# Four of the six modulation parts of each layer, computed ahead of that layer's own attention heads instead of in the layer before it and in the attention stage

## The chip, the cores and the metric

The kernel runs on one core of one Trainium2 chip, as one program. The metric is the device time of one execution in microseconds (us). A core has five engines that work side by side, each through its own queue in a fixed order: the tensor engine (PE: matmuls, with the weight loads shown apart as PEld), VectorE (DVE), ScalarE (ACT), GpSimd (POOL) and SyncE (SP), which issues every DMA transfer of this kernel. Results of PE land in PSUM banks, from which VectorE or ScalarE must take them before the bank can be used again.

## The reference, cut to what matters

Two layers of a decoder trunk over 1024 tokens of width 1024. Each layer has a mixing part (two attention branches, each of eight heads, merged by gates) and an MLP. A conditioning vector `c` gives each layer six vectors of 1024 numbers: shift, scale and gate of the mixing part, and shift, scale and gate of the MLP.

```python
c_act = jax.nn.silu(c)
for l in range(DEPTH):
    mod = (c_act @ w_ada[l] + b_ada[l])[:, None, :]
    shift1, scale1, gate1, shift2, scale2, gate2 = jnp.split(mod, N_MOD, axis=-1)
    h = _rms_norm(x, g_mix_norm[l]) * (1.0 + scale1) + shift1
    p = h @ w_in[l]
    ...
    x = x + gate1 * (merged @ w_mix_out[l])
    h = _rms_norm(x, g_mlp_norm[l]) * (1.0 + scale2) + shift2
    x = x + gate2 * (jnp.square(jax.nn.relu(h @ w_up[l])) @ w_down[l])
return _rms_norm(x, g_final)
```

`w_ada[l]` is 1024 x 6144 in f32: 24 MB for each layer, 4 MB for each of the six parts. Parts 0 and 1 (shift1, scale1) are needed at the start of the layer; part 2 (gate1) only when the merged attention output is added to x, parts 3 and 4 at the norm of the MLP, and part 5 at its end.

## The kernel before

Every f32 product is made of three matmuls on operands split into a rounded part and a rest (`hi`, `lo`): ScalarE casts the weight tile (`raw` to `parts`, `pr` to `pw`, `wr` to `ws`), GpSimd subtracts, and PE multiplies. A layer goes through these stages:

- The **front** (first part of `layer`): the norm of x, the latent projections, their norm (`lat_norm`) and rotary tables; then the projections of the first q, k, v and the first gates out of `hh`/`hl` (tiles `H`), and for p in 0 to 3 the head projections out of the latents (`lath`/`latl`, tiles `lh` and `ll`), with weights from `q_parts` and `kv_parts`. `linear` yields after each half of a job: 24 matmuls into one PSUM bank `pp`, or 9 and 6 in the head projections. There are four `pp` banks here.
- **Attention** (`attend`, two `pp` banks): eight heads of each branch, interleaved with the remaining projections (`fill`).
- The **merge**, the mixing output and the norm of the MLP.
- The **up product** (tiles `b`, `t` by weights `pw`): 14 steps of a loop over m, with seven products each, after four plain jobs.
- The **down product** (tiles `bo` by weights `ws`) in `down`, 56 steps, whose end overlaps the norm of the next layer.

The modulation sums (`modulation`) multiply c with `w_ada`. A part is four chunks of 256 columns. For each chunk four transfers of 256 KB go into the two buffers `AD`, VectorE makes eight multiply-and-add instructions into `A` (`mac`), ScalarE casts, GpSimd subtracts, and PE adds over the partitions by four matmuls of two columns (`tp<-const,A`), after which VectorE adds the bias. `modulation` is a generator: each `next` puts one transfer and two VectorE instructions in the program, so that the sums are spread over other work.

What a place in the program means is decided by `Plan`: all operations are recorded, PE's in the order of the code, and each gets a due time from PE's order; `schedule` then lays out all five queues by due time, buffers that are free, and durations that it reckons itself. The result is a fixed order for each engine. Buffers are given in turn (`AD` has two, `A` three), and a transfer that waits for its buffer holds up the transfers behind it in SyncE's queue.

Of the kernel before, what the change touches and what calls it, by code (L numbers as in the profile page):

```python
# [25 lines left out]
DEPTH = 2  # L26
# [20 lines left out]
def bc(ap):  # L47
    return ap.bitcast(F32)
# [440 lines left out]
class Trunk:  # L489
# [633 lines left out]
    def layer(self, l, xT, ssq, before):  # L1123
# [9 lines left out]
        def qkv(p):  # L1133
            qd[p], kd[p], vd[p] = self.two(), self.two(), self.dt([P, S])
            return [
                (win_w(p * P), self.keep_split(qd[p]), P),
                (win_w(512 + p * P), self.keep_split(kd[p]), P),
                (win_w(1024 + p * P), self.keep(vd[p]), P),
            ]

        def gate(m):
            gd[m] = self.dt([P, S])
            return (win_w(2208 + m * P), self.keep(gd[m], AF.Sigmoid if m < 8 else AF.Copy), P)
# [23 lines left out]
        def rope(ps, sl, n, out):  # L1167

            a, b = ltmp(), ltmp()
            nc.vector.tensor_mul(a, ps, cos[:, sl])  # L1170
            nc.vector.tensor_mul(b[:64], ps[64:], sin[64:, sl])
            nc.vector.tensor_mul(b[64:], ps[:64], sin[:64, sl])
            nc.vector.tensor_add(a, a, b)
            hi, lo = ltmp(F32R), ltmp(F32R)
            nc.scalar.copy(out=hi, in_=a)
            nc.vector.tensor_sub(lo, a, bc(hi))
            for i, t in enumerate((hi, lo)):
                for r in (0, 64) if n < 64 else (0,):
                    m = n if n < 64 else P
                    o = r // 64 * n  # L1180
                    nc.sync.dma_start(out=out[i, o : o + m, sl], in_=bc(t[r : r + m]))
# [10 lines left out]
        def lat_norm(b, tiles, width, g):  # L1192
            for hf, sl in enumerate(HALVES):
                R = self.rstd(acc[b, hf], width, ltmp)
                for i in tiles:
                    t = raw[i][:, sl]
                    nc.vector.scalar_tensor_tensor(
                        out=t, in0=t, scalar=self.v(l, g, 1, i - tiles[0]), in1=R, op0=ALU.mult, op1=ALU.mult
                    )
                    nc.scalar.copy(out=lath[i][:, sl], in_=t)  # L1200
                    nc.vector.tensor_sub(latl[i][:, sl], t, bc(lath[i][:, sl]))
# [36 lines left out]
        lat_norm(0, range(0, 3), QR, "g_q_lat")  # L1238
        lat_norm(1, range(3, 5), KVR, "g_kv_lat")
        kr_job = (kr_w, lambda ps, sl: rope(ps, sl, 16, kpe_d), P)  # L1240
        for _ in self.linear([kr_job] + qkv(0) + [gate(m) for m in range(4)], hh, hl, KT):
            pass

        c_qp, c_lt = self.vcls("qp", 16, 17, *range(18, 24)), self.vcls("lt2", 15, 5, 6, 7)

# [15 lines left out]
        def q_parts(g):  # L1261
            groups = ((0, 64), (64, 80), (80, 96))
            r = []
            for k0, k1 in ((0, 2), (2, 3)):
                r += by_heads(I["w_q_up"], k0, k1, g * 4 * QK_DIM, 4, QK_DIM, groups, c_qp)
            return r

        def kv_parts(p):
            return by_heads(I["w_kv_up"], 0, 2, 256 * p, 2, P, ((0, 64), (64, 128)), self.W["parts"])

        part = lambda w, c: lambda: [tuple(t[:, c : c + P] for t in k) for k in w]
        for p in range(4):
            mq[p], mk[p], mv[p] = self.two(), self.two(), self.dt([P, S])
            if p % 2 == 0:
                wq = q_parts(p // 2)
            q_w = part(wq, p % 2 * P)
            for _ in self.linear([(q_w, self.keep_split(mq[p], ltmp), P)], lath, latl, 3):
                pass
            wkv = kv_parts(p)
            k_w, v_w = part(wkv, 0), part(wkv, P)  # L1280
            kv_jobs = [(k_w, self.keep_split(mk[p], ltmp), P), (v_w, self.keep(mv[p]), P)]
            for _ in self.linear(kv_jobs, lath[3:], latl[3:], 2):
                pass
            if p % 2 == 0:
                g = p // 2
                qr_d[g] = self.two()
                w = part(wq, 2 * P)()
                for sl in HALVES:
                    ps = self.bank("pp")
                    self.mm3(ps, w, lath, latl, sl, 3)  # L1290
                    rope(ps, sl, 64, qr_d[g])
            for _ in self.linear([gate(4 + p)], hh, hl, KT):
                pass

        self.attention_banks()

# [67 lines left out]
        fill = [self.linear(qkv(p + 1), hh, hl, KT) for p in range(3)]  # L1364
        fill += [self.linear([gate(m) for m in range(8, 16)], hh, hl, KT)]
        fill = self.chain(fill)
        ada = self.modulation(0, [2, 3, 4, 5]) if l == 0 else iter(())
        for name, head, weights, mask, vals, steps in (
            ("sb", sb_head, self.sb_weights, self.mask_s, vd, SB_STEPS),
            ("mla", mla_head, self.mla_weights, self.mask_c, mv, MLA_STEPS),  # L1370
        ):
            if name == "sb":
                self.c_q, self.c_F = self.vcls("sq", *q_slots[:6]), self.vcls("F", *q_slots[6:])
            else:
                self.c_q = self.vcls("mq", *q_slots)
                fill = self.chain([fill, sb_out()])
            for p in range(4):
                od[name, p] = self.dt([P, S])
                a = self.attend([head(p, e) for e in range(2)], lambda: self.make_v(vals[p]), weights, mask, od[name, p])
                self.interleave(a, 19, fill, steps[p], ada)  # L1380
        for _ in self.chain([fill, ada]):
            pass


# [38 lines left out]
        steps = self.linear([(mix_w(m), update(m, 16, ssq), P) for m in range(KT)], mh, ml, KT, halves_first=True)  # L1423
# [22 lines left out]

        NP = DFF // P // 2
        hid = [self.dt([P, 8, HALF]) for m in range(NP)]
        ada = self.modulation(l + 1, range(6)) if l + 1 < DEPTH else iter(())

        def hidden(f):
            where = (0, 7) if f % 2 == 0 else (1, 2)
# [23 lines left out]
        for m in range(2, DFF // P // 2):  # L1476
            a, S3, c, d, S1, S2, S4 = self.pair_weights(I["w_up"][l, :, 2 * m * P : 2 * (m + 1) * P], c_pr, c_pw)
            u, v = self.full(c_u), self.full(c_u)
            next(ada, None)
            p1 = self.product(a, B11)  # L1480
            nc.scalar.copy(out=u[:, :HALF], in_=p1)
            p6 = self.product(S2, T[2])
            nc.vector.tensor_add(u[:, HALF:], p6, u[:, :HALF])
            next(ada, None)
            p7 = self.product(S3, T[3])
            nc.vector.tensor_add(v[:, :HALF], p7, u[:, HALF:])
            p5 = self.product(S1, T[1])
            nc.vector.tensor_add(v[:, HALF:], p5, v[:, :HALF])
            nc.vector.tensor_add(u[:, HALF:], p5, u[:, HALF:])
            next(ada, None)  # L1490
            p4 = self.product(d, T[4])
            nc.vector.tensor_sub(v[:, :HALF], v[:, :HALF], p4)
            p2 = self.product(c, B21)
            nc.vector.tensor_add(u[:, :HALF], p2, u[:, :HALF])
            next(ada, None)
            p3 = self.product(S4, B22)
            nc.vector.tensor_add(u[:, HALF:], p3, u[:, HALF:])
            for t in (v, u):
                nc.scalar.activation(out=t, in_=t, func=AF.Relu)
                nc.scalar.activation(out=t, in_=t, func=AF.Square)  # L1500
            nc.sync.dma_start(out=hid[m][:, 0], in_=u[:, :HALF])
            nc.sync.dma_start(out=hid[m][:, 1:3], in_=v.rearrange("p (a b) -> p a b", a=2))
            combine(m, u, v)
            if m in (3, 5):
                u, v = self.full(c_u), self.full(c_u)
                i = m // 2 - 1
                nc.sync.dma_start(out=u[:, :HALF], in_=hid[i][:, 0])
                nc.sync.dma_start(out=u[:, HALF:], in_=hid[i][:, 7])
                nc.sync.dma_start(out=v.rearrange("p (a b) -> p a b", a=2), in_=hid[i][:, 1:3])
                combine(i, u, v)  # L1510
        ssq = [self.tmp(), self.tmp()]
        steps = self.down(l, hid, x_d, ssq)
        for _ in range(48):
            next(steps)
            next(ada, None)
        for _ in ada:
            pass
        return self.xT, ssq, steps

    def down(self, l, hid, x_d, ssq):  # L1520
# [111 lines left out]
            yield from g  # L1632

    @staticmethod
    def interleave(a, na, b, nb, c):

        done = 0
        for i, _ in enumerate(a):
            if i % 2 == 1:
                next(c, None)  # L1640
            want = (i + 1) * nb // na
            while done < want:
                next(b, None)
                done += 1
# [69 lines left out]
```

## Time and profile before

| | |
|---|---|
| median of 3 runs | 3286.44 us (3281.02 to 3287.44) |
| the profiled execution, its own time | 3293.0 us |
| its span, first to last instruction | 3291.2 us |
| PE busy | 94% of the span |
| VectorE, ScalarE, GpSimd busy | 69%, 47%, 37% |
| mean granted clock of PE | 0.98 |

The profile is that of one execution. A busy share is an average over stages with different limits. A row of a window gives the busy time of each engine in that stretch, with the number of its instructions; the granted clock is a share of the full 2.4 GHz.

### The profile page before, as it was taken

What the parts mean: (1) busy time and instruction counts of PE and PEld (TensorE: products, weight loads), DVE (VectorE), ACT (ScalarE), POOL (GpSimd) and SP (SyncE); (2) the same over time, 40 slices, a digit from 0 to 9 for tenths busy, and PEclk for the clock granted to TensorE, in tenths of its full rate; (3) what the DMA queues carried; (4) which work ended last, traced back from release to release, by engine and by line L of the source; (5) the groups of instructions that cost most, each with busy time, mean ns of one, the idle gap of its engine ahead of it and who ended that gap; (6) DMA issues with size and microseconds to landing.
All of it is one profiled execution on the core that took longest, in us unless ns stands there. A gap on an engine that the chain in (4) does not pass through costs nothing. (4 is left out here: it accounts for less than half of the span.)

```text
span 3291.2 us, 42785 instructions
## 1 busy us (share of the span) xinstructions
PE 3103.3 (94%) x14823; PEld 2510.8 (76%) x14823; DVE 2258.7 (69%) x3238; ACT 1544.9 (47%) x2643; POOL 1229.2 (37%) x952
## 2 busy tenths in 40 slices
PE   5999999999998898999989999999999989999998
PEld 4877777788776776777777877778887767888786
DVE  7453677678667778799986225656766777558886
ACT  4443555566444443433344225666654444444334
POOL 3222444111244544345433223441113455544442
PEclk9999999999999999999999999999999999999999
DMA  6446456555843654876332474444466435467522
GB/s 219 151 146 202 136 151 164 140 139 171 271 140 103 200 194 161 281 226 199 99 122 76 139 221 125 130 117 124 101 213 208 141 114 196 154 226 225 179 77 90
DMA packets 450268, 532.45 MB, mean 162 GB/s; under 512 B 32498, under 2 KB 320900, under 8 KB 450052
## 3 DMA queue, kind: packets, MB, share of 16 engines
q1 hardware_dynamic: 450052, 529.72, 52.7%
q8 instruction: 117, 1.92, 0.3%
q14 instruction: 99, 0.81, 0.1%
HBM read 367.60 MB, written 162.00 MB: 161 GB/s over the span
## 5 line engine op out<-in xcount | busy, mean ns | idle before, releaser
L213 PE MATMUL pp<-H,parts 128*128 128x512 f32 x4032 | 1060.2, 407 | 10.5 <-ACT H L213 8.9
L213 PEld LDWEIGHTS pp<-H,parts 128*128 128x128 f32 x4032 | 741.0, 191 | 162.7 <-ACT H L213 10.4
L213 PE MATMUL pp<-bo,ws 128*128 128x512 f32 x2688 | 645.6, 401 | 31.3 <-POOL ws L213 15.0
L213 POOL TENSOR_TENSOR parts<-raw,parts 128x1024 fp32r<-128x1024 f32 (+2 forms) x168 | 370.7, 2208 | 721.2 <-ACT parts L213 681.5
L213 PEld LDWEIGHTS pp<-bo,ws 128*128 128x128 f32 x2688 | 508.4, 191 | 155.5 <-POOL ws L213 18.1
L213 POOL TENSOR_TENSOR ws<-wr,ws 128x1024 fp32r<-128x1024 f32 x112 | 297.1, 2662 | 368.7 <-ACT ws L213 342.0
L213 PE MATMUL pp<-t,pw 128*128 128x512 f32 x1344 | 323.4, 398 | 10.7 <-ACT u L213 10.0
L213 PEld LDWEIGHTS pp<-t,pw 128*128 128x128 f32 x1344 | 251.5, 189 | 71.8 <-ACT u L213 11.2
L213 ACT CAST parts<-raw 128x1024 fp32r<-128x1024 f32 (+2 forms) x168 | 151.9, 904 | 242.1 <-PE pp L213 202.2
L213 PE MATMUL pp<-b,pw 128*128 128x512 f32 x1008 | 246.8, 402 | 12.4 <-DVE u L213 12.4
L213 DVE TENSOR_TENSOR wtl<-tp,wth 128x512 fp32r<-128x512 f32 (+3 forms) x384 | 207.0, 550 | 67.3 <-ACT wth L213 65.6
L213 DVE SCALAR_TENSOR_TENSOR A<-AD,const,A 128x256 f32<-128x256 f32 x280 | 223.3, 797 | 26.6 <-DMA AD<-in_w_ada 23.2
L213 POOL TENSOR_TENSOR pw<-T,pw 128x512 fp32r<-128x512 f32 x112 | 162.3, 1464 | 208.4 <-ACT pw L213 194.4
L213 ACT CAST wth<-tp 128x512 fp32r<-128x512 f32 (+3 forms) x384 | 181.1, 481 | 125.2 <-PE tp L213 120.5
L213 DVE TENSOR_TENSOR_SCAN F<-F,sc 128x128 f32<-128x128 f32 (+7 forms) x128 | 171.7, 1349 | 99.1 <-ACT F L213 74.2
L213 DVE SCALAR_TENSOR_TENSOR x<-pp,const,x 128x512 f32<-128x512 f32 x256 | 181.7, 741 | 80.0 <-PE pp L213 80.0
L213 PEld LDWEIGHTS pp<-b,pw 128*128 128x128 f32 x1008 | 190.4, 191 | 59.5 <-DVE u L213 14.8
L213 POOL TENSOR_TENSOR W<-W,F 128x127 f32<-128x127 f32 (+7 forms) x128 | 155.2, 1217 | 209.7 <-ACT W L213 122.8
L213 ACT CAST bo<-T 128x512 fp32r<-128x512 f32 x224 | 135.3, 619 | 185.8 <-DMA T<-dram 124.4
L213 DVE TENSOR_TENSOR bo<-T,bo 128x512 fp32r<-128x512 f32 x224 | 201.4, 946 | 18.3 <-ACT bo L213 17.9
L213 PE MATMUL tp<-const,W 128*128 128x128 f32 x1152 | 185.1, 274 | 17.8 <-DVE wtl L213 9.8
L213 ACT ACTIVATE u<-u 128x1024 f32<-128x1024 f32 x112 | 118.7, 1060 | 149.1 <-DVE u L213 142.6
(151 smaller groups left out, 4620.6 us busy)
## 6 DMA issues: line engine op xcount, KB each, us to landing
T<-dram SPq DMA_DIRECT2D x352, 256.0 KB
dram<-T SPq DMA_DIRECT2D x208, 256.0 KB
dram<-u SPq DMA_DIRECT2D x92, 512.0 KB
AD<-in_w_ada SPq DMA_DIRECT2D x160, 256.0 KB
raw<-in_w_in SPq DMA_DIRECT2D x70, 512.0 KB
wr<-in_w_down SPq DMA_DIRECT2D x64, 512.0 KB
pr<-in_w_up SPq DMA_DIRECT2D x56, 512.0 KB
sq<-dram SPq DMA_DIRECT2D x96, 256.0 KB
```

The source lines that it names most:

```text
L213: getattr(getattr(nc, engine), method)(*[r(x) for x in a], **{n: r(x) for n, x in k.items()})
```

## The change

Parts 2 to 5 of layer 0 were spread over layer 0's attention, and all six parts of layer 1 over layer 0's up and down products. Now parts 2 to 5 of each layer are spread over that layer's own front, from the q, k, v projections to the last head projection; parts 0 and 1 of layer 1 stay in layer 0's up product, and the attention stages and the down product have none. In the up product there are now three `next` calls in each step in place of four.

```diff
@@ -1238,8 +1238,10 @@
+        ada = self.modulation(l, [2, 3, 4, 5])
         for _ in self.linear([kr_job] + qkv(0) + [gate(m) for m in range(4)], hh, hl, KT):
-            pass
+            next(ada, None)
+            next(ada, None)
...
             for _ in self.linear([(q_w, self.keep_split(mq[p], ltmp), P)], lath, latl, 3):
-                pass
+                next(ada, None)
...
             for _ in self.linear(kv_jobs, lath[3:], latl[3:], 2):
-                pass
+                next(ada, None)
...
                     rope(ps, sl, 64, qr_d[g])
+                    next(ada, None)
             for _ in self.linear([gate(4 + p)], hh, hl, KT):
-                pass
+                next(ada, None)
+                next(ada, None)
+        for _ in ada:
+            pass
...
-        ada = self.modulation(0, [2, 3, 4, 5]) if l == 0 else iter(())
...
-                self.interleave(a, 19, fill, steps[p], ada)
-        for _ in self.chain([fill, ada]):
+                self.interleave(a, 19, fill, steps[p])
+        for _ in fill:
             pass
...
-        ada = self.modulation(l + 1, range(6)) if l + 1 < DEPTH else iter(())
+        ada = self.modulation(l + 1, range(2)) if l + 1 < DEPTH else iter(())
...
-            next(ada, None)
             p4 = self.product(d, T[4])
...
+        for _ in ada:
+            pass
         for _ in range(48):
             next(steps)
-            next(ada, None)
-        for _ in ada:
-            pass
```

What this does to the queues is shown at three places.

First, VectorE's queue in layer 0's front, at the head projections of p = 0. `lt<-pp,lt` takes the rest of a q or k projection out of its bank, `lt<-pp,cs` is the start of the rotary step. Before:

```order
L213 TENSOR_TENSOR lt_319_1690<-pp_1668,lt_318_1685 128x512
L213 TENSOR_TENSOR lt_322_1708<-pp_1683,lt_321_1703 128x512
L213 TENSOR_TENSOR lt_328_1735<-pp_1701,lt_327_1717 128x512
L213 TENSOR_TENSOR lt_331_1751<-pp_1713,lt_330_1742 128x512
L213 TENSOR_TENSOR lt_338_1773<-pp_1749,cs_1184 128x512
```

And of the change:

```order
L213 TENSOR_TENSOR lt_380_1805<-pp_1774,lt_379_1793 128x512
L213 SCALAR_TENSOR_TENSOR A_1748<-AD_1770,const_98,A_1748 128x256
L213 TENSOR_TENSOR lt_387_1822<-pp_1791,lt_386_1815 128x512
L213 TENSOR_SCALAR A_1836<-AD_1796,const_98 128x256
L213 SCALAR_TENSOR_TENSOR A_1836<-AD_1796,const_98,A_1836 128x256
L213 TENSOR_TENSOR const_277<-tp_1828,const_252 128x2
L213 SCALAR_TENSOR_TENSOR A_1836<-AD_1830,const_98,A_1836 128x256 x2
L213 TENSOR_TENSOR lt_395_1871<-pp_1813,lt_394_1838 128x512
L213 SCALAR_TENSOR_TENSOR A_1836<-AD_1854,const_98,A_1836 128x256 x2
L213 TENSOR_TENSOR lt_399_1899<-pp_1832,lt_398_1882 128x512
L213 TENSOR_TENSOR lt_413_1908<-pp_1877,cs_1184 128x512
```

The five evacuations of PSUM banks, which followed each other, now have one to four instructions of the sums between them, each of which waits for its own transfer into `AD`.

Second, VectorE's queue in layer 0's down product. `x<-pp,const,x` adds a product to x, `wr` forms a weight combination. Before:

```order
L213 SCALAR_TENSOR_TENSOR A_13085<-AD_12968,const_98,A_13085 128x256
L213 TENSOR_TENSOR wr_12839<-wr_12413,wr_12839 128x1024
L213 SCALAR_TENSOR_TENSOR A_13085<-AD_13112,const_98,A_13085 128x256
L213 SCALAR_TENSOR_TENSOR x_12563<-pp_13114,const_277,x_12563 128x512
L213 SCALAR_TENSOR_TENSOR A_13085<-AD_13112,const_98,A_13085 128x256
L213 SCALAR_TENSOR_TENSOR x_12563<-pp_13114,const_277,x_12563 128x512
L213 SCALAR_TENSOR_TENSOR A_13085<-AD_13147,const_98,A_13085 128x256
L213 SCALAR_TENSOR_TENSOR x_12756<-pp_13114,const_277,x_12756 128x512
```

And of the change:

```order
L213 SCALAR_TENSOR_TENSOR x_12308<-pp_12864,const_277,x_12308 128x512 x2
L213 SCALAR_TENSOR_TENSOR x_12494<-pp_12864,const_277,x_12494 128x512 x2
L213 TENSOR_TENSOR wr_12586<-wr_12279,wr_12586 128x1024
L213 TENSOR_TENSOR wr_12427<-wr_12427,wr_12586 128x1024
L213 SCALAR_TENSOR_TENSOR x_12378<-pp_12897,const_277,x_12378 128x512 x2
```

The evacuations now follow each other without the sums between them.

Third, SyncE's queue in layer 0's front, around the loads of the head projections' weights (`raw<-in_w_kv_up`). Before:

```order
L213 DMA raw_1567<-in_w_kv_up 128x2x256
L213 DMA raw_1577<-in_w_in 128x8x128
L213 DMA dram_1585<-T_1572 128x512
L213 DMA dram_1585<-T_1606 128x512
L213 DMA raw_1621<-in_w_kv_up 128x2x256
```

And of the change:

```order
L213 DMA raw_1605<-in_w_kv_up 128x2x256
L213 DMA AD_1612<-in_w_ada 128x2x256
L213 DMA raw_1624<-in_w_in 128x8x128
L213 DMA AD_1635<-in_w_ada 128x2x256
L213 DMA dram_1581<-lt_1622 16x512 x2
L213 DMA dram_1581<-lt_1630 16x512
L213 DMA AD_1654<-in_w_ada 128x2x256
L213 DMA dram_1581<-lt_1630 16x512
L213 DMA dram_1671<-T_1616 128x512
L213 DMA AD_1685<-in_w_ada 128x2x256
L213 DMA dram_1671<-T_1675 128x512
L213 DMA raw_1697<-in_w_kv_up 128x2x256
```

Four transfers of the sums now stand between two weight loads and the stores of the projections.

Counted over the whole order, the groups of four small matmuls stand before: 16 in layer 0's attention, 13 in its up product, 11 in its down product. After: 14 in layer 0's front (the first 568 other matmuls ahead of the first score) and 2 just behind the first score, over 630 matmuls; 8 in its up product, one for every 112 other matmuls where it was one for every 84; and 16 in layer 1's front, over 635 matmuls. In both up and down products the order of PE's other matmuls stays as it was.

## Rows read from the trace of the kernel before

**Rows 1.** Page, busy us of each engine, share of the span, instructions.

```profile
PE 3103.3 (94%) x14823; PEld 2510.8 (76%) x14823; DVE 2258.7 (69%) x3238; ACT 1544.9 (47%) x2643; POOL 1229.2 (37%) x952
```

**Rows 2.** Tiles' PE instructions: count, ns min/median/max, first and last start in us.

```profile
L213 PE MATMUL sc<-sq,sq x192: 274/390/776, 304.6 to 570.1; 128*128 128x512 f32 x96, 128*128 128x256 f32 x64, 128*128 128x384 f32 x32
L213 PE MATMUL pp<-merged,parts x384: 388/394/503, 893.9 to 989.2; 128*128 128x512 f32 x192
L213 PE MATMUL pp<-b,pw x504: 387/395/797, 1051.2 to 1361.3; 128*128 128x512 f32 x168
...
L213 PE MATMUL sc<-sq,sq x192: 274/390/509, 1967.3 to 2220.1; 128*128 128x512 f32 x96, 128*128 128x256 f32 x64, 128*128 128x384 f32 x32
L213 PE MATMUL pp<-merged,parts x384: 387/394/499, 2523.9 to 2615.9; 128*128 128x512 f32 x192
L213 PE MATMUL pp<-b,pw x504: 387/394/400, 2678.6 to 2953.3; 128*128 128x512 f32 x168
```

**Rows 3.** Windows, both layers: busy PE, PEld, DVE, ACT, POOL; clock, DMA share, GB/s.

```profile
304.60:893.90 589.30, 556.12 (x3153) 456.26 (x3152) 418.36 (x786) 339.48 (x690) 173.50 (x235) 0.99 0.59 167
1967.30:2523.90 556.60, 540.23 (x3089) 447.48 (x3088) 354.27 (x648) 336.04 (x676) 162.35 (x219) 0.99 0.53 150
1051.20:1361.50 310.30, 288.22 (x1228) 231.05 (x1227) 232.23 (x320) 124.94 (x185) 152.67 (x112) 0.97 0.58 189
2678.60:2953.50 274.90, 273.91 (x1177) 220.26 (x1177) 173.80 (x220) 126.88 (x179) 147.34 (x100) 1.00 0.54 179
```

**Rows 4.** Windows of tile bo alone, down product: PE, PEld, DVE, ACT; clock, DMA.

```profile
1361.50:1629.30 267.80, 245.68 (x990) 188.04 (x989) 68.65 (x85) 53.41 (x88) 0.96 0.63 200
1629.30:1723.20 93.90, 86.07 (x355) 68.55 (x355) 19.93 (x23) 10.81 (x18) 0.95 0.31 104
2953.50:3191.90 238.40, 233.95 (x1005) 188.32 (x1006) 87.92 (x88) 52.90 (x86) 1.00 0.56 177
```

**Rows 5.** Windows of the fronts, columns as in rows 3.

```profile
150.00:172.60 22.60, 22.12 (x95) 17.58 (x95) 18.41 (x28) 12.33 (x19) 4.81 (x2) 1.00 0.57 180
172.60:304.60 132.00, 131.99 (x568) 106.17 (x568) 47.20 (x68) 45.70 (x81) 32.59 (x33) 1.00 0.59 180
1790.00:1967.30 177.30, 177.20 (x763) 142.65 (x762) 61.98 (x92) 56.25 (x99) 43.07 (x37) 1.00 0.52 159
```

**Rows 6.** PE's waits: up, down (layer 0), up (layer 1), whole span: total, times, longest.

```profile
PE pp L213 <- DVE u L213: 13.1, 8, 3.2
...
PE pp L213 <- POOL ws L213: 12.6, 5, 5.1
...
PE pp L213 <- ACT u L213: 1.0, 2, 0.7
...
PE tp L213 <- ACT A L213: 1.0, 2, 0.5
```

**Rows 7.** Timeline of PE, a group of four small matmuls: start, length, instruction.

```profile
1053.99 0.50 PE L213 MATMUL tp<-const,A 128*128 128x2 f32 x4
1054.35 5.85 PE L213 MATMUL pp<-t,pw 128*128 128x512 f32 x24
```

**Rows 8.** Windows of tile A alone, attention and up: PE, PEld, DVE, ACT, POOL.

```profile
304.60:893.90 589.30, 11.23 (x64) 10.72 (x64) 75.77 (x125) 6.58 (x16) 12.23 (x16) 0.99 0.59 167
...
1051.20:1361.50 310.30, 8.43 (x51) 9.57 (x51) 77.95 (x92) 4.70 (x12) 8.86 (x12) 0.97 0.58 189
```

**Rows 9.** Tiles A and raw: instructions, ns min/median/max, first and last start.

```profile
L213 DVE SCALAR_TENSOR_TENSOR A<-AD,const,A x280: 449/484/2760, 35.0 to 1625.8; 128x256 f32<-128x256 f32 x140
...
L213 POOL TENSOR_TENSOR parts<-raw,parts x168: 732/2394/11578, 19.5 to 2665.6; 128x1024 fp32r<-128x1024 f32 x120, 128x512 fp32r<-128x512 f32 x32, 128x256 fp32r<-128x256 f32 x16
```

**Rows 10.** Timeline of the sums' transfers; VectorE's idle time ended by them, whole span.

```profile
1541.02 3.43 SPq L213 DMA_DIRECT2D AD<-in_w_ada  x2
1544.93 1.00 DVE L213 SCALAR_TENSOR_TENSOR A<-AD,const,A 128x256 f32<-128x256 f32 x2 [0.88 <-DMA AD<-in_w_ada]
...
  DMA AD<-in_w_ada: 23.2, 17
```

More of the change, by code (lines that the diff above doesn't have):

```diff
@@ L1634, in interleave @@
     @staticmethod
-    def interleave(a, na, b, nb, c):
+    def interleave(a, na, b, nb):
         done = 0
         for i, _ in enumerate(a):
-            if i % 2 == 1:
-                next(c, None)
             want = (i + 1) * nb // na
```

## The prediction

> **What bounds the kernel now.** I read the busy times first. The tensor engine (PE) is busy for 3103 of 3291 us [rows 1], so the time can only fall where PE waits or runs at a lower clock. I then cut the trace by stage, because the two layers run the same program except for one thing: layer 0 carries all the modulation sums that the change moves, layer 1 carries none. Layer 1 is therefore a measurement of layer 0 without the sums. The stage borders are the first and last starts of PE's matmul groups [rows 2]: attention from the first score matmul to the first matmul on the merged tiles, the up product over its own matmuls up to the next start 0.2 us later, and the down product from there.
>
> The reader is to see this in the stages [rows 3]. Attention takes 589.3 us in layer 0 and 556.6 us in layer 1, with 3153 against 3089 matmuls: the 64 more are those of the sums. The up product takes 310.3 against 274.9 us, and in layer 1 PE is busy for 273.9 of the 274.9. In the down product 990 matmuls take 267.8 us while the sums run; in layer 1 1005 take 238.4 us, that is 234.8 us for 990, and the granted clock is 0.96 against 1.00 [rows 4]. By contrast the two fronts, where the sums are to go, hold PE at 131.99 of 132.0 and 177.2 of 177.3 us [rows 5].
>
> The list of waits says who holds PE up: in layer 0's up product it is VectorE's results (13.1 us), in its down product the weight split of GpSimd (12.6 us), and in layer 1's up product 1.0 us in all [rows 6]. For the sums' own tiles PE waits 1.0 us; what it waits for is VectorE and GpSimd work that stands among them.
>
> **The change, part by part.** A part of the modulation is four chunks. A chunk is four transfers of 256 KB, eight VectorE instructions, a ScalarE cast, a GpSimd subtraction and one group of four small matmuls. Before, layer 0's attention has 16 chunks, the up product 13 and the down product 11; after, the order has them at 2, 8 and 0. Layer 0's front gets 14 (the last two groups stand just behind the first score) and layer 1's front 16.
>
> *The matmuls themselves.* A group starts at 1053.99 and the next matmul at 1054.35 us [rows 7]: 0.36 us. This is moved and not saved.
>
> *Attention, layer 0.* 589.3 - 556.6 = 32.7 us for 16 chunks, of which 16 x 0.36 = 5.8 are PE's own and 26.9 are waits. Fourteen leave: 32.7 x 14/16 = **28.6 us**.
>
> *Up product, layer 0.* 310.3 - 274.9 = 35.4 us for 13 chunks, 2.7 each. Five leave. The eight that stay stand one per 112 matmuls instead of one per 84, so at the same price per chunk 13.6 us come back; if the eight cost only their matmuls, 35.4 - 2.9 = 32.5 us. The row is that of the same instructions at nearly the same density, so I stay near it: **16 us**.
>
> *Down product, layer 0.* All 11 chunks leave. Upper end 267.8 - 234.8 = 33.0 us. Lower end: only the time in which PE was not at a down matmul comes back, (267.8 - 245.7) - (238.4 - 234.0) = 17.7 us. The clock of 0.96 belongs to the waits, and layer 1 shows the stage without them at 1.00: I take **31 us**. The stretch after the last sum, from 1629.3 us, runs at 0.95 without any sum [rows 4]; it belongs to the next layer's norm and stays.
>
> *The two fronts.* They pay 14 x 0.36 = 5.0 and 16 x 0.36 = 5.8 us on PE. What hides the rest is slack: a linear job gives a PSUM bank every 24 matmuls, 24 x 132.0/568 = 5.6 us, and there are four, so VectorE may be some ten us late before PE feels it; in the head projections a bank lasts only 9 or 6 matmuls, 2.1 or 1.4 us. VectorE's load decides. The mean of one sum instruction is 75.77/125 = 0.61 us in attention and 77.95/92 = 0.85 us in the up product [rows 8], with a median of 0.48 everywhere [rows 9]. GpSimd is busy for 32.6/132 = 25% of the front, 29% of attention and 49% of the up product, so attention is nearest: 128 x 0.61 = 78 us for each front. Layer 0's front already has 18.4 + 47.2 us of VectorE in 154.6 us, so it comes to 144, or 93%; layer 1's has 62.0 and comes to 140 of 177.3, or 79%. The transfers add 0.59 x 589.3 - 0.53 x 556.6 = 53 us of DMA time per 16 chunks: 78 + 46 = 124 of 132 us in layer 0's front, which is nearly full. Bounds of the stall: nothing (PE never waits there now) and the rate of attention, 26.9/16 = 1.7 us a chunk, 27 us in each front. Attention has VectorE at 71%, the fronts more, but with deeper slack; I take **10 us** in layer 0, where the latent norms and rotary tables already fill VectorE, and **5 us** in layer 1.
>
> The stretched instructions show the mechanism: one sum instruction takes 449 ns at least and 2760 at most, GpSimd's weight split 2394 ns at the median and 11578 at most [rows 9]. The Trainium skill, page "SBUF — State Buffer", section "SBUF: two separate sides", says that VectorE and GpSimd share a port pair which one of them holds for a whole instruction, and that a VectorE instruction with two SBUF inputs contends with a GpSimd one that reads SBUF; the trace agrees. An estimate by that page: with GpSimd there 25% of the time and half of 2.4 us to wait, an instruction would take 0.48 + 0.30 = 0.78 us, layer 0's front would need 166 of 154.6 us, and the sum below would shrink by some 11 us to about 39.
>
> *The sum.* 28.6 + 16 + 31 = 75.6 us come back; 5.0 + 5.8 + 10 + 5 = 25.8 us are paid. Net 49.8. The profiled execution took 3293.0 us (span 3291.2), so 3243.2; the median of the runs shown is 6.6 us below that execution, so **3237 us**.
>
> **The rivals.** *Fronts without stall, a clean up product.* 28.6 + 32.5 + 33.0 - 10.8 = 83 us, or 3203 us. For it: PE's full fronts. Against it: VectorE at 93%.
>
> *The fronts take attention's stall on themselves.* 27 us in each: 75.6 - 10.8 - 54 = 11 us gain, 3276 us. For it: the VectorE load; the head projections with their short banks. Against it: four banks, and attention has two.
>
> *The transfers can't keep up (slower).* There are two AD buffers, and a chunk is two rounds through them. In layer 0's down product a pair of transfers is issued from 1541.02 us, VectorE waits for the first and starts at 1544.93: 3.9 us to land, and then two instructions, 1.0 us [rows 10]. Two such rounds take 9.8 us; the order gives a chunk about 39 matmuls, 9.2 us. That is 10 us late per front, my stall. PE's order holds the groups at fixed places and VectorE's order holds the evacuations behind the sums, so a later landing is paid on PE at once. The gain of 64.8 us left after the matmuls is eaten when the 32 chunks are 2.0 us late each, at a landing of 4.6 us. At 5 us it is 32 x 2.8 = 90 us and the kernel takes 3286 + 25 = 3311 us. The DMA share of 0.94 that I work out speaks for it; that VectorE's waits for AD come to 23.2 us in all for 40 chunks speaks against. The Trainium skill, page "DMA: Bandwidth & Descriptors", section "Latency and other measured facts", gives 0.2 us of memory latency on average and 2 us at high load. By an estimate from that page a landing of 3.9 us could rise to 5.7, past the point of 4.6; the trace of before has no such transfers in a front to show it.
>
> *The change does not do what it says.* If layer 0's stages are longer for another reason than the sums, only matmuls move: 3286 us. For it: the stretch without sums at a clock of 0.95. Against it: the layers run the same matmuls, and the excess of layer 0 is there in each of the three stages that have sums and not in the front, which has none.
>
> **How the numbers follow.** Forecast (3218 to 3256 us) 0.60; clean fronts 0.13; stall as in attention 0.15; transfers too late 0.07; no effect 0.05. The range leaves out half of the clean case, the last two cases and the upper edge of the third: 3206 to 3270 us. 0.2% is 6.6 us, about what a measurement of this kernel can tell from no change; a twentieth or so of the third case and all of the last fall within it: faster 0.86, same 0.07, slower 0.07.
>
> **What would show it.** Right: layer 0's attention at 560 to 565 us, its up product at 290 to 298, the down stretch of 990 matmuls at 234 to 238 with a clock of 0.99 or more; layer 0's front some 15 us longer and layer 1's some 11, with waits of PE for VectorE's evacuations and little for the sums. Wrong: waits of VectorE for AD in the fronts beyond 20 us each, PE waiting for the sums' tiles there, score matmuls held up by late head loads, or an up product that keeps its 310 us.

## The result, and the profile after

| | before | changed |
|---|---|---|
| median of 4 runs, us | 3285.94 | 3248.05 (3243.55 to 3261.27) |
| ratio, 95% interval | | 0.9889 (0.9868 to 0.9910) |
| the profiled execution, us | 3293.0 | 3261.27 |
| its span, us | 3291.2 | 3259.3 |

The kernel is 37.9 us faster where 49 were forecast. The profiled execution of the changed kernel is the slowest of its four, 13 us above the median, so its stages are rather long.

First the same starts of PE's matmul groups as in [rows 2], in the changed kernel (instructions, count, ns min/median/max, first and last start):

```profile
L213 PE MATMUL sc<-sq,sq x192: 274/390/686, 335.6 to 592.1; 128*128 128x512 f32 x96, 128*128 128x256 f32 x64, 128*128 128x384 f32 x32
L213 PE MATMUL pp<-merged,parts x384: 388/394/503, 895.2 to 990.8; 128*128 128x512 f32 x192
L213 PE MATMUL pp<-b,pw x504: 387/395/774, 1053.4 to 1345.5; 128*128 128x512 f32 x168
L213 PE MATMUL pp<-bo,ws x1344: 387/394/795, 1345.7 to 1669.7; 128*128 128x512 f32 x192
...
L213 PE MATMUL sc<-sq,sq x192: 275/388/502, 1938.6 to 2186.2; 128*128 128x512 f32 x96, 128*128 128x256 f32 x64, 128*128 128x384 f32 x32
```

From such starts comes the account by stage on which everything below rests. The columns are: start of the first score of layer 0 (what its front costs), layer 0's attention, its up product, its down product (first to last start), layer 1's front (from that last start to its first score), layer 1's attention. Every line is worked out from one profiled execution. Layer 1's attention, which holds no sums in twelve of the fourteen kernels of this document, takes from 543.0 to 556.6 us in their profiled executions, so a difference of a few us between two stages of that length is not told apart from this spread.

| us | first score | attention 0 | up 0 | down 0 | front 1 | attention 1 |
|---|---|---|---|---|---|---|
| before | 304.6 | 589.3 | 310.3 | 361.5 | 244.3 | 556.6 |
| changed | 335.6 | 559.6 | 292.3 | 324.0 | 268.9 | 551.0 |
| difference | +31.0 | -29.7 | -18.0 | -37.5 | +24.6 | -5.6 |

So 85 us came back where I had reckoned with 75.6, and 55.6 were paid where I had reckoned with 25.8. The windows of the changed kernel, with the columns of [rows 3]: attention, up and down product of layer 0, then the head projections of layer 0 and of layer 1, from their first matmul to the first score:

```profile
335.60:895.20 559.60, 542.91 (x3098) 448.18 (x3097) 364.03 (x671) 336.08 (x677) 164.61 (x222) 0.99 0.55 154
1053.40:1345.70 292.30, 282.31 (x1209) 227.53 (x1208) 199.98 (x277) 127.17 (x187) 152.11 (x107) 0.98 0.56 188
1345.70:1669.90 324.20, 314.96 (x1347) 253.26 (x1346) 282.80 (x305) 133.61 (x184) 142.32 (x55) 0.99 0.50 161
221.00:335.60 114.60, 103.60 (x434) 82.35 (x433) 65.85 (x118) 33.01 (x63) 27.90 (x32) 0.94 0.83 252
1825.90:1938.60 112.70, 102.29 (x436) 81.55 (x436) 64.08 (x113) 32.32 (x63) 28.47 (x32) 0.95 0.84 258
```

The same head projections in the kernel before the change, which filled PE:

```profile
212.50:304.60 92.10, 92.09 (x397) 74.17 (x396) 24.93 (x36) 29.15 (x53) 21.28 (x23) 1.00 0.71 215
1875.50:1967.30 91.80, 91.80 (x397) 74.12 (x396) 24.70 (x36) 29.17 (x53) 21.42 (x23) 1.00 0.70 214
```

They became 22.5 and 20.9 us longer. VectorE is busy in them for 57% only, and the granted clock falls to 0.94 and 0.95. Who waits there is told by the list of waits of the changed kernel (total us, times, longest), for layer 0's front from 150 us on, PE and then VectorE, and the same for layer 1's front from 1740 us on:

```profile
PE tp L213 <- ACT A L213: 13.0, 6, 3.5
PE pp L213 <- DVE lt L213: 2.0, 1, 2.0
...
DVE A L213 <- DMA AD<-in_w_ada: 37.1, 25, 4.2
...
PE tp L213 <- ACT A L213: 10.8, 7, 2.9
...
DVE A L213 <- DMA AD<-in_w_ada: 37.1, 27, 3.6
```

PE waits above all for the sums' own tiles; for VectorE's evacuations there is one wait of 2.0 us in layer 0. VectorE in turn waits 74 us in the two fronts for transfers into AD, where the whole program had 23.2 us of such idle time before [rows 10]. One such round, from the timelines of SyncE and of VectorE (start, length, engine, instruction, wait before it):

```profile
260.03 2.41 SPq L213 DMA_DIRECT2D AD<-in_w_ada  x2
...
267.01 0.70 DVE L213 TENSOR_SCALAR A<-AD,const 128x256 f32<-128x256 f32 x1 [2.55 <-DMA AD<-in_w_ada]
```

A pair is issued, its first at 260.03 us, and VectorE, which stands idle for 2.55 us, can start on that first one at 267.01: 7.0 us, against 3.9 in [rows 10]. This round is one of the longest. The trace also holds the time at which each transfer has raised its semaphore (the counter that tells of its landing) in full. From issue to there the 36 transfers into AD in layer 0's head projections take 4.0 us at the median (mean 4.5, from 2.6 to 8.1) and the 31 in layer 1's 4.0 us (mean 3.9, at most 6.1); the 40 in layer 0's down product of the kernel before take 3.1 us (mean 3.5).

**The theories.** *A, transfers:* two AD buffers are filled too slowly, VectorE waits in its fixed order, and PE, whose order holds the groups of small matmuls at fixed places, pays. *B, work:* the sums' VectorE time is too much for the front, as I had argued. *C, load:* the DMA engines are too full there, and other transfers come late. Two more came up on the way: *D*, the three A buffers chain one chunk to the next; and that the planner's times for the sums are too short, so that it puts the groups ahead of their data in any place.

### The profile page after: what moved, and what is told of

It is laid out like the page before. It is cut to its first block, busy times and chain, and to the rows that moved or that the text cites. A ratio compares the mean times of both kernels' runs of the same rounds, so it can differ in the third digit from the quotient of the medians.

```text
span 3259.3 us, 42862 instructions
## 1 busy us (share of the span) xinstructions
PE 3097.0 (95%) x14823; PEld 2508.9 (77%) x14823; DVE 2246.9 (69%) x3238; ACT 1547.7 (47%) x2643; POOL 1225.6 (38%) x952
## 5 line engine op out<-in xcount | busy, mean ns | idle before, releaser
L213 PE MATMUL pp<-bo,ws 128*128 128x512 f32 x2688 | 628.7, 395 | 12.5 <-DVE bo L213 5.0
L213 DVE SCALAR_TENSOR_TENSOR A<-AD,const,A 128x256 f32<-128x256 f32 x280 | 195.9, 700 | 73.7 <-DMA AD<-in_w_ada 68.3
L213 DVE TENSOR_TENSOR_SCAN F<-F,sc 128x128 f32<-128x128 f32 (+7 forms) x128 | 171.4, 1347 | 97.4 <-ACT F L213 72.3
L213 DVE TENSOR_TENSOR bo<-T,bo 128x512 fp32r<-128x512 f32 x224 | 207.5, 973 | 15.8 <-ACT bo L213 15.4
L213 ACT CAST ws<-wr 128x1024 fp32r<-128x1024 f32 x112 | 116.9, 1049 | 188.2 <-PE pp L213 174.6
```

Source lines behind the costliest of these rows:

```text
L213: getattr(getattr(nc, engine), method)(*[r(x) for x in a], **{n: r(x) for n, x in k.items()})
```

## The experiments

Twelve kernels ran, each beside the kernel before; ratios are to it.

| | median, us | ratio | 95% interval |
|---|---|---|---|
| changed kernel | 3248.05 | 0.9889 | 0.9868 to 0.9910 |
| no_transfer | 3222.18 | 0.9818 | 0.9794 to 0.9842 |
| unread_transfer | 3236.69 | 0.9858 | 0.9840 to 0.9875 |
| half_sums | 3235.69 | 0.9854 | 0.9837 to 0.9872 |
| four_buffers | 3233.63 | 0.9850 | 0.9831 to 0.9869 |
| layer0_only | 3276.91 | 0.9985 | 0.9974 to 0.9996 |
| layer1_only | 3256.82 | 0.9916 | 0.9895 to 0.9937 |
| true_costs | 3214.96 | 0.9793 | 0.9770 to 0.9815 |
| no_transfer_five_a | 3221.94 | 0.9803 | 0.9779 to 0.9827 |
| before_true_costs | 3256.12 | 0.9920 | 0.9906 to 0.9935 |
| true_costs_four | 3217.16 | 0.9801 | 0.9784 to 0.9817 |
| true_landing | 3212.87 | 0.9786 | 0.9770 to 0.9803 |
| true_vector | 3234.94 | 0.9855 | 0.9840 to 0.9870 |

Each of these kernels is laid out anew by `Plan`, so its order changes together with what its edit names. Counted in the traces, no_transfer, unread_transfer, half_sums, four_buffers and no_transfer_five_a have all 16 groups of small matmuls ahead of layer 0's first score, one for every 32 to 33 other matmuls, where the change has 14 there and one for every 42. In layer 1 it is one for every 41 against 42. So layer 0's fronts in these five carry two groups more than the change's.

**no_transfer and unread_transfer.** The sums of the fronts read tiles of the hidden state; in the second kernel the transfers are still made.

```diff
-                        self.mac(acc, w[:, k, :], k0 + k)
+                        src = w[:, k, :] if m < 2 else bc(self.hh[k0 + k][:, HALVES[0]])[:, :256]
+                        self.mac(acc, src, k0 + k)
```

> The sums of parts 2 to 5 in both fronts are multiplied out of tiles of the hidden state that lie in SBUF, so their 128 transfers from w_ada fall away; VectorE's, ScalarE's, GpSimd's and PE's instructions stay (the modulation is then wrong, this part of the computation is replaced). Theory A (VectorE waits for the transfers, through two buffers, and PE pays): the waits go, the first score of layer 0 starts at 308 to 316 us in place of 335.6, layer 1's front takes 248 to 256 us in place of 268.7, the kernel 3248 - 40 = about 3208 us. Theory B (VectorE's work in the fronts is too much): nothing goes, 3240 to 3250 us. Theory C (the DMA engines are full in the fronts): as A, about 3208 us.

> As no_transfer, but the 128 transfers are still made into the same two buffers and no one reads them (parts 2 to 5 of the modulation are again formed from the hidden state). DMA load stays, VectorE's wait for it goes. Theory A: as without transfers, 3205 to 3218 us. Theory B: 3240 to 3250 us. Theory C: the load is there, so 3240 to 3250 us, with PE held by late weights or late head loads.

Both are faster than the changed kernel, by 26 and 11 us, and neither reaches the 3208 us of theory A. In the stages the head projections take 102.4 and 102.0 us without transfers and 102.5 and 100.4 us with unread ones, against 114.6 and 112.7: there the waits for the transfers are worth 11 to 12 us in each layer, and their load nothing, which for this stage is A and not C. But 10 of the 22 us remain without any transfer. Over the whole kernel it is less clear: the 3236.69 us of unread_transfer lie between the ranges of A and of C. The two profiled executions are 17.2 us apart; the first score differs by 3.9 us and layer 1's front by 0.8, and most of the rest is 6.6 us in layer 0's attention and 6.0 us in its down product, whose instructions are the same. I can't put that to anything, so what the load costs outside the head projections stays open. The head projections of layer 0 in no_transfer, and PE's wait for the sums' tiles that is left in that front:

```profile
219.40:321.80 102.40, 98.26 (x438) 78.12 (x437) 66.02 (x122) 32.95 (x64) 29.34 (x33) 1.00 0.62 195
...
PE tp L213 <- ACT A L213: 7.7, 6, 2.5
```

**half_sums.** All transfers, half of the sums' VectorE work in the fronts.

```diff
-                    for k in range(2):
+                    for k in range(2 if m < 2 else 1):
```

> All transfers stay, but only the first of the two rows of each transfer of parts 2 to 5 is added, so half of the sums' VectorE work in the fronts falls away (half of each of these sums is left out). Theory A: a round through a buffer is shorter by one instruction of 0.48 us of about 4.9, so at most 10 us in all come back: 3236 to 3248 us, and VectorE's waits for AD stay at 30 us or more in each front. Theory B: 39 us of VectorE work less in each front gives back half of the 45 us of stall or more: 3215 to 3225 us. Theory C: no change, 3248 us.

12 us came back, half of what theory B wanted and just over what A allowed. VectorE's waits for AD stayed at 39.8 and 35.8 us, and the head projections at 111.0 and 109.1. Where it helped is ahead of them: layer 0's first head projection starts at 216.7 us in place of 221.0 (212.5 before). In that stretch, where latent norm and rotary tables already keep VectorE busy, work counts; in the head projections half of it is worth 3.6 us in each layer.

**four_buffers.** Four AD buffers in the fronts; two 2 KB tiles of an evacuation now share one 4 KB buffer.

```diff
-        c_qp, c_lt = self.vcls("qp", 16, 17, *range(18, 24)), self.vcls("lt2", 15, 5, 6, 7)
+        c_qp, c_lt = self.vcls("qp", 16, 17, *range(18, 24)), self.vcls("lt2", 15, 5)
+        AD = self.cls("AD", ["ad0", "ad1"] + ([self.V[6], self.V[7]] if parts[0] == 2 else []))
```

> Four AD buffers in the fronts in place of two. The space comes from the evacuations of the head projections and rotary steps, whose two 2 KB tiles share one 4 KB buffer. All is computed. Theory A: four transfers under way at a time, a chunk is one round and not two; VectorE's waits for AD fall from 37 us in each front to under 12, and 25 to 40 us come back: 3208 to 3223 us. Theory B: no change, 3243 to 3253 us. Theory C: no change or a loss, as the engines are full: 3245 to 3260 us.

The waits for AD went as expected, to 1.5 and 0.8 us, but only 14 us came back. VectorE's and PE's rows of layer 0's front, from 150 us on:

```profile
DVE A L213 <- DMA AD<-in_w_ada: 1.5, 2, 0.9
...
PE tp L213 <- ACT A L213: 8.2, 8, 2.8
```

So VectorE's wait for the transfers is gone and PE still waits for the sums' tiles. With more buffers the planner also moved the groups closer together: in layer 0's front one for every 32 other matmuls, where the change has one for every 42. In layer 1 they stand nearly as in the change; there PE's waits for the sums' tiles fall from 10.8 to 4.9 us and the head projections from 112.7 to 103.9 us. Theory A as I had it was not enough. My reading was that the buffers set how fast a chunk can come, but that the order, which again puts the groups ahead of the data, decides what PE loses by it; true_costs and the kernels after it test that.

**layer0_only and layer1_only.** Each half of the change alone: layer 0's, and with `l == 1` in the same line layer 1's, with the sums of the other half where they were before.

```diff
-        ada = self.modulation(l, [2, 3, 4, 5])
+        ada = self.modulation(l, [2, 3, 4, 5]) if l == 0 else iter(())
```

> Only layer 0's parts 2 to 5 move from its attention to its front; all six parts of layer 1 stay in layer 0's MLP as before. All is computed. Theory A (a stall of the front as large as the wait that leaves attention, measured at 26 us against 27): layer 0's front 30 us longer, its attention 30 us shorter, up and down products as before: 3278 to 3294 us, no change. Rival (the fronts' stall in the changed kernel comes from both layers' moves together, or was large only in the slow profiled execution): 3262 to 3275 us.

> Only layer 1's parts 2 to 5 move from layer 0's MLP to layer 1's own front; layer 0's stay in its attention. All is computed. Theory A: the up and down products give back 18 + 37 us, layer 1's front pays 25, so nearly the whole gain of the change: 3243 to 3257 us. Rival (both moves gain about the same): 3262 to 3270 us.

Layer 0's move is worth 0.15%: its first score is 29.0 us later and its attention 35.3 us shorter. Layer 1's is worth 0.84%: up and down products are 15.8 and 37.1 us shorter, layer 1's front 22.0 us longer and its attention 6.4 shorter. The median of layer0_only lies just below, that of layer1_only just inside what theory A gave. Three quarters of the gain comes from the part of the change that empties the MLP. That layer 0's first score is 29.0 us later here, 31.0 in the change, speaks against the rival too: the stall of the front needs neither both moves nor the slow profiled execution of the change.

**true_costs.** The planner is told 0.6 us for a VectorE instruction of the sums and 1.5 us more until a transfer into AD has landed. Only the order differs.

```diff
+        mine = {v.tile.cls.name for v in outs}
+        op.extra = 1.5 if op.eng == "DMA" and "AD" in mine else 0.0
+        if op.eng == "DVE" and "A" in mine:
+            op.dur = 0.6
-                        end = now + 1.2 + dur
+                        end = now + 1.2 + dur + op.extra
```

> The change with the planner told longer times for the sums: 0.6 us for a VectorE instruction of the sums (it reckons 0.35 to 0.40) and 1.5 us more until a transfer into AD has landed. The work is the same, only the order differs: PE's groups stand later, one per 55 to 60 matmuls in place of 40, and four of them pass into layer 0's attention. All is computed. Theory A (two buffers can't be filled faster, and PE's order holds the groups ahead of the data): PE's waits for the sums' tiles fall from 13 and 11 us to under 4 each, the head projections take 98 to 104 us in place of 113 to 115, and 10 to 20 us come back: 3228 to 3238 us. Theory B (VectorE's work itself): no change, 3243 to 3253 us.

33 us faster than the changed kernel, more than expected. The head projections take 100.4 and 105.2 us, PE's waits for the sums' tiles are 3.4 and 3.6 us as expected, and the up product, where 283.1 us stand in place of 292.3, gained too, which I had not expected. Not all of it is a better place in the front: in the trace three groups of each layer have passed from its front into its attention (5 stand there in layer 0 where the change has 2, and 3 in layer 1 where it has none).

**no_transfer_five_a.** no_transfer with five A buffers in the fronts.

```diff
+        A = self.cls("A", ["a0", "a1", "a2"] + ([self.V[6], self.V[7]] if parts[0] == 2 else []))
```

> As no_transfer, with five A buffers in the fronts in place of three (the space comes as in four_buffers), so that a chunk's sums need not wait until the chunk before has passed ScalarE, GpSimd and PE. Parts 2 to 5 of the modulation are formed from the hidden state. Theory D (what is left of the stall without transfers, some 7 us in the head projections of each layer beside PE's own 3, is that chain of buffers): the head projections take 95 to 98 us in place of 102, and 3205 to 3214 us. Theory B (it is VectorE's work and the evacuations behind it): no change, 3217 to 3227 us.

The median is that of no_transfer. In layer 1 the head projections take 97.4 us, as theory D says, in layer 0 100.7 us, as it does not. What the chain of A buffers costs is a few us at most and is not settled.

**before_true_costs.** The kernel before the change, with the edit of true_costs.

> The kernel before the change, with the planner told the longer times of the sums as in true_costs (0.6 us for a VectorE instruction, 1.5 us more until a transfer into AD has landed). All is computed. Theory P (the place of the sums matters: the attention and the MLP of layer 0 have VectorE as second bound, whatever the order): 3272 to 3286 us, and true_costs keeps 1.6% or more ahead of it. Rival (it is the planner's too short times that cost, in any place): 3225 to 3250 us, and most of the gain of the change could have been had without moving anything.

It lies between the two: 0.8% faster than before, with layer 0's attention 13.3 us, its up product 8.7 and its down product 5.6 us shorter. The too short times cost in any place. Put together, the four kernels make a square: with the planner's own times the move is worth 1.1%, with the longer times 0.9920 to 0.9793, 1.3%; the times are worth 0.8% without the move and 1.0% with it. Both expectations missed the time; the first part of theory P holds, that the place matters by itself, but its lead is 1.3% and not 1.6%.

**true_costs_four, true_landing and true_vector.** true_costs with four buffers; and each of its two times alone.

> true_costs and four_buffers together. All is computed. Theory A: four buffers let the plan keep PE's groups inside the front (16 over 580 matmuls, as in the change) and the longer times keep them behind the data: 3205 to 3216 us, the same as true_costs or up to 10 us below it. Rival (the two remedies fill the same gap, and more transfers at once crowd the front): 3216 to 3230 us.

> The change with the planner told only the longer landing of the transfers into AD (1.5 us more); its times for VectorE's sums stay at 0.35 to 0.40 us. All is computed. If the landing is what the plan had wrong in the fronts (theory A), most of the gain of true_costs is here: 3214 to 3228 us, the up product stays at 292 us. If it was VectorE's time (theory B), 3238 to 3250 us.

> The change with the planner told only the longer VectorE time of the sums (0.6 us); the landing stays as it was reckoned. All is computed. Theory A: VectorE's waits for AD in the fronts stay at 25 us or more each, but the groups stand one per 45 matmuls and not one per 40, so a part comes back: 3228 to 3242 us. Theory B: 3213 to 3223 us, all of the gain of true_costs, with the up product at 283 us.

The longer landing alone gives 0.9786, all of the gain of true_costs; its median is the lowest here, but not clear of that of true_costs. The longer VectorE time alone gives 0.9855, and VectorE's waits for AD stay at 32.3 and 44.1 us in the fronts, with the up product at 283.8 us (291.0 with the longer landing alone). So the up product's gain belongs to VectorE's time. Layer 1's front gains by the landing: 253.4 us, against 266.5 with the longer VectorE time and 268.9 in the change. In layer 0 either of the two brings the first score forward, to 320.3 and 321.8 us from 335.6, and the two can't be told apart. More buffers add nothing to true_costs. They also suggest that the longer times help at the same density, by an amount not far above the spread of a stage: true_costs_four has 16 groups in layer 1's front, one for every 42 other matmuls as in the change, and that front takes 257.0 us, where four_buffers takes 263.9. With the landing told, VectorE's and PE's waits in layer 0's front from 150 us on, and a window that begins 3.6 us ahead of layer 1's head projections and ends 0.5 us behind them (columns of [rows 3]):

```profile
DVE A L215 <- DMA AD<-in_w_ada: 19.3, 10, 4.1
...
PE tp L215 <- ACT A L215: 7.5, 5, 3.2
```

```profile
1794.50:1895.20 100.70, 99.72 (x447) 80.50 (x447) 54.06 (x103) 32.30 (x61) 27.62 (x31) 1.00 0.86 267
```

The transfers, the buffers and the sums are the same, and a transfer takes no less time to land (4.1 and 4.2 us at the median in the head projections of the two layers). VectorE still waits for AD, at a DMA share of 0.86, but in layer 1 PE is busy for 99.7 of 100.7 us at a clock of 1.00 (PE waits 1.3 us in that front for the sums' tiles), and the head projections themselves take 96.6 us. The groups now stand one per 53 other matmuls in layer 1's front instead of one per 42, behind their data, and two of the 16 have passed into layer 1's attention, which takes 553.1 us (551.0 in the change). This is shown for layer 1; in layer 0's front a wait for the sums' tiles ahead of the head projections stays (3.2 us, 3.5 in the change), and two groups more pass into its attention, which at 553.2 us is no longer for it.

## Why the prediction was right, and where its steps were wrong

*The comparison of the layers* held. Attention gave 29.7 us (28.6 forecast), the up product 18.0 (16), and the down product 37.5 (31). There the lower end of 17.7 us was no use: the clock came back with the waits, 1.00 in place of 0.96 over the matmuls of [rows 4], as I had taken it. That layer 1's attention would become 5.6 us shorter I did not forecast; layer0_only, which leaves layer 1 as it was, shows 4.0 as well, and both lie within the spread of this stage.

*The two fronts* are the term that was mis-sized: 31.0 and 24.6 us in place of 15.0 and 10.8. Less the small matmuls the stall is 26.0 and 18.8 us where I took 10 and 5. In layer 0 that is the size I gave to the third case, attention's rate carried into both fronts (27 each), and in layer 1 it is nearer to it than to the forecast. That the time still came within the range is in part luck. The three stages gave 9.6 us more than reckoned, which made good a third of the 29.8 us by which I had the fronts too cheap. And the range reached up into the third case: 75.6 - 55.6 = 20 us of gain, or 3266 us, would have lain in it as well.

*The reason* was wrong where it matters. I let VectorE's load decide, 93% of layer 0's front. That figure charged the front with the 128 instructions of 16 chunks, though 14 chunks stand there; with 112 it is 134 of 154.6 us, 87%. And the load does not decide in the head projections, where most of the stall is: VectorE is busy there for 57%, and halving the sums changes them by 4 us. Ahead of them, in layer 0, it counts (half_sums). The mean of a sum instruction in layer 0's front is 0.62 us (61.87 us for 100), just as estimated. The row that the estimate by the Trainium skill's page "SBUF — State Buffer" (section "SBUF: two separate sides") would have needed is not there: it asked for 0.78 us.

*The rival with the transfers* had the mechanism. I worked out 3.9 us of landing, 10 us late per front, and set the point at which it decides at 4.6 us. VectorE's waits for AD, 37.1 us in each front (over 20), and PE's waits for the sums' tiles are signs that I had named for being wrong, and both came. It did not end on the slower side: the mean landing in the head projections, 4.5 and 3.9 us, stayed short of 4.6, and of the 74 us of such waits PE saw 24 us as waits for the sums' tiles. That the chunks under way hide the rest is argued and not shown. The Trainium skill's page "DMA: Bandwidth & Descriptors", section "Latency and other measured facts", names 0.2 us of memory latency on average and 2 us at high load. The trace agrees in direction, and at the median within that size: 4.0 us of landing at a DMA share of 0.83 in layer 0's head projections, against 3.1 us at 0.63 in the down product of the kernel before.

*The signs.* The up product (292.3) fell in the interval that I gave, attention (559.6) just beside it, and the down product ran at a clock of 1.00 at the same matmuls, 987 in 231.3 us, a little faster than I gave:

```profile
1345.70:1577.00 231.30, 229.36 (x987) 185.01 (x987) 80.81 (x86) 52.46 (x86) 1.00 0.59 189
```

The sign for the fronts, PE waiting for VectorE's evacuations and little for the sums, was the wrong way round: 2.0 us for the former and 13.0 for the latter in layer 0.

What stays open: 10 us in layer 0's front that no kernel removed (first score at 314.9 us at best, 5 us of it the small matmuls), the part of the stall in the head projections that is left without transfers, and the difference between no_transfer and unread_transfer outside the fronts.

## What to carry to other kernels

When two layers run the same program and only one carries some extra work, the difference of their stages prices that work at once, clock included; it was right here within some 20% for each stage, where the price of the new place, read from busy shares, was less than half of what it proved to be (25.8 against 55.6 us). Work that is moved into a full stage brings its own chain of transfers, buffers and instructions, and where the order of each engine is fixed, the time between two uses of its buffers has to be compared with a landing measured under that stage's load, and over many transfers rather than one. If a planner sets that order, tell it such a time before moving anything: this one number was worth 1.0%, about as much as the move (1.1%).

## What the runs showed of the hardware that was not expected

Some waits of PE cost about twice their length, because the clock falls behind them, and others cost only their length. In the changed kernel, the timeline of PE behind the longest wait for the sums in the head projections (start, length, instruction):

```profile
288.01 0.37 PE L213 MATMUL tp<-const,A 128*128 128x2 f32 x1 [3.07 <-ACT A L213]
288.24 0.77 PE L213 MATMUL pp<-lh,parts 128*128 128x512 f32 x1
288.81 0.63 PE L213 MATMUL pp<-ll,parts 128*128 128x512 f32 x1
289.24 0.63 PE L213 MATMUL pp<-lh,parts 128*128 128x512 f32 x1
...
293.72 0.88 PE L213 MATMUL pp<-lh,parts 128*128 128x512 f32 x2
294.44 0.39 PE L213 MATMUL pp<-ll,parts 128*128 128x512 f32 x1
294.66 0.62 PE L213 MATMUL pp<-lh,parts 128*128 128x512 f32 x2
```

From 288.81 to 289.24 one matmul takes 0.43 us, the lower of the two clock levels (512 columns at 1.2 GHz), and from 294.44 on the usual 0.23. The thirteen matmuls in between took 2.7 us more than at that pace, after a wait of 3.07 us. In layer 1's head projections a wait of nearly the same length has no such price:

```profile
1841.65 0.27 PE L213 MATMUL tp<-const,A 128*128 128x2 f32 x1 [2.92 <-ACT A L213]
1841.78 0.47 PE L213 MATMUL pp<-ll,qp 128*128 128x512 f32 x1
1842.10 0.62 PE L213 MATMUL pp<-lh,qp 128*128 128x512 f32 x2
1842.56 0.39 PE L213 MATMUL pp<-ll,qp 128*128 128x512 f32 x1
```

Two matmuls from 1842.10 take 0.46 us, which is the usual pace, and the granted clock from 1841.6 to 1853.0 us is 1.00. The length of a wait alone does not tell which of the two will follow; what does is open.

Over layer 0's head projections the account is nearly closed. PE is idle for 11.0 us (114.6 - 103.6), and the clock is at its lower level for 13.7 us in all, which at half the pace costs 6.8 us and makes the mean clock of 0.94. With some 3 us for the small matmuls that is 21 of the 22.5 us by which they became longer. So idle time and clock together cost about 1.6 times the idle time.
